# Two plain units of weights instead of three after each block of seven products

## The chip, the cores and the metric

One core of a Trainium2 chip runs the whole kernel. The metric is the device time of one execution in microseconds; three runs of the kernel before were timed, and one execution was profiled.

## The reference

A decoder trunk of two layers over 256 tokens of width 2048, in float32. Layer 0 mixes tokens with stick-breaking attention, layer 1 with a gated DeltaNet; a SwiGLU feed-forward of hidden width 5632 follows each. The change lies in the feed-forward alone:

```python
D_MODEL = 2048; SEQ = 256; DEPTH = 2; FFN_HIDDEN = 5632

def swiglu(h, w_gu, w_down):
    gate, up = jnp.split(h @ w_gu, 2, axis=-1)
    return (jax.nn.silu(gate) * up) @ w_down

for i in range(DEPTH):
    x = x + mixer(rms_norm(x, mix_norm[i]))          # mixer by layer
    x = x + swiglu(rms_norm(x, ffn_norm[i]), ffn_w_gu[i], ffn_w_down[i])
```

## The kernel before

**Units.** Weights come from HBM in units of 256 rows by 512 columns (`Unit`, `UK = 2` tiles of 128 rows; one load of 512 KB). A unit belongs to a `Block`, which is 512 columns of a product with all its rows. TensorE multiplies in fp32r, so each operand is split in a high and a low part: ScalarE writes the high part (L328), VectorE subtracts it from the raw weights and writes the low part (L332). This is a unit's conversion. TensorE then makes three products for each tile (high by high, high by low, low by high; L354).

**Two kinds of unit in the feed-forward.** A *plain unit* needs 12 matmuls of 512 columns. Its conversion is one instruction of 1024 columns on ScalarE and one on VectorE; in the profile it is named `slabs<-slab`. The gate and up products of six of the eleven column groups (`SEVEN`) are made in a form of Strassen's method with seven products of half size instead of eight; such a *seven unit* needs 21 matmuls of 256 columns. VectorE first forms sums of quarters of the weights (`sums`: one instruction of 512 columns and two of 256, `w<-w`); its conversion is 1792 columns on ScalarE and on VectorE, for every second one in two pieces of 768 and 1024 (`w<-w,w`). A block of seven products has eight seven units, and twelve such blocks (gate and up in turn) make 96 seven units in a layer; I number them 1 to 12.

**The end of such a block.** The results lie in four PSUM banks, `acc` two times and `bank` two times, which the next block of seven products uses again. They are drained by `quarters`: one ScalarE copy (`slab<-acc`, 256 columns) and four VectorE additions (`slab<-acc,slab` and `slab<-bank,slab`). Behind a gate block ScalarE applies silu; behind an up block VectorE multiplies gate and up (`slab<-slab,rstd`), transposes twice (L939), and transfers through HBM finish the transposition. Plain blocks (the other column groups, and the down projection) use the remaining banks; theirs are products with `rstd` from a bank, transposes, and additions into `x`.

**Buffers.** Plain units have two raw and two converted buffers, seven units three raw and two converted ones (each then converted alternately in one and in two pieces). A converted buffer is free when TensorE has finished the unit in it. Conversions are written into the engines' queues in the order of the units, up to three units ahead (`AHEAD`), sums up to five ahead (`SUMS`).

**The order.** `ffn_units` makes the lists of the seven units and of the plain ones; the first 13 plain units stand first (`LEAD + BEFORE`), and `merge` finds the order of the rest, 96 seven and 155 plain ones, as the cheapest path through all orders by costs: for a seven unit that follows the end of a block of seven products with `gs` plain units between, for two seven units in a row, for more than three plain ones in a row, and for a distance from 1.3 plain units to each seven unit (`RATIO`). `gs` counts up to three. The resulting order sets the queue of every engine, TensorE's first; a planner in the program (`tick`, `spend`) lets the smaller tasks (drains, silu, transposes) into the queues by its own account of times. Then each engine works through its queue in order and waits on semaphores.

Of the kernel before, what the change touches and what calls it, by code (L numbers as in the profile page):

```python
# [157 lines left out]
class Trunk:  # L158
# [867 lines left out]
    def merge(self, s, o):  # L1026


        ns, no = len(s), len(o)
        ends = [u.last for u in s]  # L1030
        best = {(0, 0, 0, 1, 3): (0.0, None)}
        layer = best
        trail = []
        for _ in range(ns + no):
            nextl = {}
            for st, (cost, _p) in layer.items():
                i, j, kind, run, gs = st

                for k in (0, 1):
                    ii, jj = i + k, j + 1 - k  # L1040
                    if ii > ns or jj > no or (k and kind == 1 and run >= 2):
                        continue
                    c = cost
                    if k:
                        c += 4.0 * max(0, 2 - gs) + (1.0 if gs == 2 else 0)
                        c += 0.3 * (kind == 1)
                        g2 = 0 if ends[i] else 3
                    else:
                        g2 = min(3, gs + 1)
                    r = min(run + 1, 4) if k == kind else 1  # L1050
                    if not k and r > 3 and ii < ns:
                        c += 2.0
                    if ii < ns:
                        c += 0.15 * max(0.0, abs(jj - self.RATIO * ii) - 1.5)
                    key = (ii, jj, k, r, g2)
                    if key not in nextl or nextl[key][0] > c:
                        nextl[key] = (c, st)
            trail.append(nextl)
            layer = nextl
        st = min(layer, key=lambda q: layer[q][0])  # L1060
        order = []
        for nextl in reversed(trail):
            order.append(st[2])
            st = nextl[st][1]
        return order[::-1]
# [727 lines left out]
```

## Time and profile before

| | |
|---|---|
| runs | 2709.22, 2709.37, 2713.18 us (median 2709.37) |
| profiled execution | 2705.98 us, span 2704.3 us |
| granted TensorE clock | 1.000 |
| read from HBM, over the span | 508.20 MB, 197 GB/s read and written |
| seven units, layer 0 (plain ones between them) | about 440 to 1037 us of the span |
| seven units, layer 1 | about 2020 to 2619 us |

In the profile PE is TensorE's matmul, PEld its weight load, DVE VectorE, ACT ScalarE, SP the engine that issues the loads. A row of a timeline gives the start in us from the span's start, the length in us (of equal neighbours merged, with their count), engine, line, operation, what is written and read, and in brackets the idle time before it and who ended it. A row of windows gives for each engine the busy time and the number of instructions.

### The profile page before, as it was taken

Reading aid. Unit: us, or ns where it says so; the run is one execution under the profiler, and the core shown is the slowest. Engines: PE = TensorE matmul, PEld = TensorE weight load, DVE = VectorE, ACT = ScalarE, POOL = GpSimd, SP = SyncE. Lnnn points to the kernel's source line nnn. Section 1 sums busy time; section 2 is a strip of 40 time slices with the busy share of each in tenths; the row PEclk is TensorE's granted clock in tenths of the full one; section 3 lists DMA queues with packets and bytes.
Section 4 is the critical chain, followed back from the end, with each engine's and each line's share of the span. In section 5 each row is a group of like instructions: output and inputs, shape, how many; then the busy total and the mean of one; then the engine's idle time right before and its main releaser. Section 6 shows DMA issues by size and latency. Waiting matters only on the chain.

```text
span 2704.3 us, 39527 instructions
## 1 busy us (share of the span) xinstructions
PE 2669.4 (99%) x14730; PEld 2274.6 (84%) x14730; DVE 2182.7 (81%) x3451; ACT 1491.8 (55%) x1961; POOL 11.2 (0%) x95
## 2 busy tenths in 40 slices
PE   9999999999999999999999999999999999999999
PEld 7888888888888888888888888888878888888887
DVE  6556568899999897678778887887679899989885
ACT  6555556554555554565665556645575555555453
POOL 0000000000000000000000000000000000000000
PEclk9999999999999999999999999999999999999999
DMA  7766775787676777855656556556567767767776
GB/s 245 202 185 196 219 211 164 208 231 212 203 218 205 208 211 233 227 174 172 182 143 195 159 161 175 168 153 186 170 191 212 223 196 220 217 188 218 226 209 188
DMA packets 487611, 534.41 MB, mean 198 GB/s; under 512 B 188087, under 2 KB 267258, under 8 KB 487418
## 3 DMA queue, kind: packets, MB, share of 16 engines
q1 hardware_dynamic: 487370, 531.87, 67.1%
q8 instruction: 115, 1.88, 0.3%
q14 instruction: 78, 0.64, 0.1%
q10 hardware_dynamic: 48, 0.02, 0.0%
HBM read 508.20 MB, written 23.59 MB: 197 GB/s over the span
## 4 chain that ended last, share of the span: by engine, by line
PE 83%; DVE 10%; issue 2%; ACT 2%; DMA 2%; SPq 0%; ACTq 0%; DVEq 0%
PE acc L354 61%; PE bank L354 20%; DVE w L332 5%; DVE slabs L332 2%; PE bank L363 1%; DMA slab<-in_ffn_w_gu_dram 1%; ACT slabs L328 1%; ACT w L328 1%; DVE slab L338 1%; DVE slab L332 1%; DVE slab L939 1%; DMA slab<-in_ffn_w_down_dram 0%; ACT slab L328 0%; DVE x L332 0%; DMA w<-in_ffn_w_gu_dram 0%
## 5 line engine op out<-in xcount | busy, mean ns | idle before, releaser
L332 DVE TENSOR_TENSOR w<-w,w 128x1024 fp32r<-128x1024 f32 (+2 forms) x746 | 946.3, 1285 | 249.0 <-ACT w L328 247.6
L328 ACT ACTIVATE w<-w 128x1024 fp32r<-128x1024 f32 (+2 forms) x650 | 802.8, 1244 | 417.8 <-PE acc L354 347.0
L354 PE MATMUL acc<-w,hTh 128*128 128x512 f32 (+1 forms) x3232 | 925.0, 369 | 9.1 <-DVE w L332 8.4
L354 PEld LDWEIGHTS acc<-w,hTh 128*128 128x128 f32 x3232 | 585.9, 189 | 120.5 <-DVE w L332 14.5
L354 PE MATMUL acc<-w,hTl 128*128 128x512 f32 (+1 forms) x1616 | 590.2, 365 | 3.1 <-DVE hTl L338 3.1
L328 ACT ACTIVATE slabs<-slab 128x1024 fp32r<-128x1024 f32 x264 | 279.3, 1058 | 431.9 <-DMA slab<-in_ffn_w_gu_dram 123.8
L332 DVE TENSOR_TENSOR slabs<-slab,slabs 128x1024 fp32r<-128x1024 f32 x264 | 321.5, 1218 | 93.1 <-ACT slabs L328 93.1
L354 PE MATMUL acc<-w,kh 128*128 128x512 f32 x1184 | 369.6, 393 | 0.0
L354 PEld LDWEIGHTS acc<-w,hTl 128*128 128x128 f32 x1616 | 304.5, 188 | 53.5 <-DVE hTl L338 3.9
L332 DVE TENSOR_TENSOR w<-w 128x256 f32<-128x256 f32 (+1 forms) x576 | 291.2, 508 | 9.8 <-DMA w<-in_ffn_w_gu_dram 2.6
L354 PEld LDWEIGHTS acc<-w,kh 128*128 128x128 f32 x1184 | 218.8, 188 | 43.7
L354 PE MATMUL acc<-w,kl 128*128 128x512 f32 x592 | 230.7, 390 | 0.0
L354 PE MATMUL acc<-slabs,hTh 128*128 128x512 f32 x608 | 190.1, 392 | 2.8 <-DVE slabs L332 2.8
L354 PE MATMUL bank<-w,wide 128*128 128x256 f32 x1296 | 178.9, 283 | 0.0
L354 PEld LDWEIGHTS bank<-w,wide 128*128 128x128 f32 x1296 | 165.8, 192 | 0.0
L354 PE MATMUL bank<-slabs,hTh 128*128 128x512 f32 x512 | 159.9, 392 | 3.1 <-DVE slabs L332 3.1
L354 PE MATMUL bank<-slabs,kh 128*128 128x512 f32 x512 | 159.6, 392 | 3.4 <-DVE slabs L332 3.4
L354 PE MATMUL acc<-slabs,kh 128*128 128x512 f32 x480 | 149.9, 392 | 2.1 <-DVE slabs L332 1.9
L354 PEld LDWEIGHTS acc<-slabs,hTh 128*128 128x128 f32 x608 | 111.0, 188 | 25.1 <-DVE slabs L332 4.9
L354 PEld LDWEIGHTS acc<-w,kl 128*128 128x128 f32 x592 | 111.1, 188 | 23.4
L354 PE MATMUL acc<-slabs,hTl 128*128 128x512 f32 x304 | 118.3, 389 | 0.0
L328 ACT ACTIVATE slab<-bank 32x128 f32<-32x128 f32 (+4 forms) x181 | 67.9, 379 | 89.3 <-PE bank L354 87.1
(216 smaller groups left out, 2933.4 us busy)
## 6 DMA issues: line engine op xcount, KB each, us to landing
w<-in_ffn_w_gu_dram SPq DMA_DIRECT2D x212, 512.0 KB, 4.5
slab<-in_ffn_w_gu_dram SPq DMA_DIRECT2D x140, 512.0 KB, 4.5
w<-in_gdn_w_in_dram SPq DMA_DIRECT2D x129, 512.0 KB, 4.3
slab<-in_ffn_w_down_dram SPq DMA_DIRECT2D x124, 512.0 KB, 4.5
w<-in_sb_w_in_dram SPq DMA_DIRECT2D x96, 512.0 KB, 4.5
w<-in_gdn_w_in_dram SPq DMA_DIRECT2D x128, 256.0 KB, 3.7
w<-in_gdn_w_out_dram SPq DMA_DIRECT2D x64, 512.0 KB, 4.4
w<-in_ffn_w_down_dram SPq DMA_DIRECT2D x52, 512.0 KB, 5.5
```

The costliest lines, as they stand in the source:

```text
L328: self.nc.scalar.activation(out, in_, func, **kw)
L332: self.nc.vector.tensor_tensor(out, a, b, op=op)
L338: self.nc.vector.scalar_tensor_tensor(out, a, s, b, op0=op0, op1=op1)
L354: self.nc.tensor.matmul(out, lhsT, rhs, start=start, stop=stop, skip_group_check=True)
L363: self.nc.tensor.transpose(out, in_, self.ident[:p, :p])
L939: self.nc.vector.transpose(s, t)
```

## The change

```diff
@@ -1042,7 +1042,7 @@ merge
                     c = cost
                     if k:
-                        c += 4.0 * max(0, 2 - gs) + (1.0 if gs == 2 else 0)
+                        c += 4.0 * max(0, 2 - gs)
                         c += 0.3 * (kind == 1)
                         g2 = 0 if ends[i] else 3
```

A seven unit after exactly two plain units behind a block's end no longer costs anything. In the order that `merge` finds, with p a plain and s a seven unit, the blocks 2 to 6 then read (blocks 1 and what follows 12 are as before):

```text
block  before               after
2      pppspspspspspspsps   ppsppspspsppspspsps
3      pppspspsppspspspsps  ppspspsppspspspsps
4      pppspspspspspspsps   ppsppspspspsppspsps
5      pppspspsppspspspsps  ppspspsppspspspsps
6      pppspspspspspspsps   ppspsppspspspspsps
```

All eleven blocks from 2 to 12 begin with three plain units before and with two after, in both layers; the third is found later in the block. The numbers of both kinds of unit are the same.

Two places show what this does to the queues. First VectorE at the end of block 2 in layer 0, before: the row of `slabs` with 1024 columns is a plain conversion (here that of the third plain unit of block 3), the one with 1792 columns the conversion of the first seven unit of block 3, the rows with `acc_104`, `bank_108` and `bank_110` are the drain.

```order
L338 SCALAR_TENSOR_TENSOR slab<-acc_106,rstd_141,slab 128x512
L338 SCALAR_TENSOR_TENSOR slab<-acc_107,rstd_141,slab 128x512
L332 TENSOR_TENSOR w_2928<-w_2928 128x512
L332 TENSOR_TENSOR slab<-acc_104,slab 128x512
L332 TENSOR_TENSOR w_2928<-w_2928 128x256
L332 TENSOR_TENSOR slab<-bank_108,slab 128x512
L332 TENSOR_TENSOR w_2928<-w_2928 128x256
L332 TENSOR_TENSOR slab<-bank_110,slab 128x2x256
L332 TENSOR_TENSOR slab<-bank_108,slab 128x256
L939 STREAM_TRANSPOSE slab<-slab 128x512 x2
L332 TENSOR_TENSOR slabs<-slab,slabs 128x1024
L332 TENSOR_TENSOR w_123<-w_122,w_123 128x1792
```

The same place after; the first `slabs` row is now the conversion of the second plain unit of block 3, the last that of the third.

```order
L332 TENSOR_TENSOR slabs<-slab,slabs 128x1024
L332 TENSOR_TENSOR w_2928<-w_2928 128x256 x2
L332 TENSOR_TENSOR w_123<-w_122,w_123 128x1792
L332 TENSOR_TENSOR slab<-acc_104,slab 128x512
L332 TENSOR_TENSOR slab<-bank_108,slab 128x512
L332 TENSOR_TENSOR slab<-bank_110,slab 128x2x256
L332 TENSOR_TENSOR slab<-bank_108,slab 128x256
L332 TENSOR_TENSOR w_122<-w_122 128x512
L332 TENSOR_TENSOR slabs<-slab,slabs 128x1024
L332 TENSOR_TENSOR w_122<-w_122 128x256 x2
L332 TENSOR_TENSOR w_123<-w_2928,w_123 128x768
L332 TENSOR_TENSOR w_2927<-w_122,w_123 128x1024
```

The conversion of the first seven unit stood behind the drain and the third plain conversion; now it stands ahead of the drain, and the third plain conversion behind it. The two products with `acc_106` and `acc_107` and the two transposes, of a plain up block that ends there, have moved up, ahead of the second plain conversion.

On ScalarE the same place reads before as follows (the 256 columns of `acc_105` are the drain's copy):

```order
L328 ACTIVATE w_123<-w_122 128x1792
L328 ACTIVATE slabs<-slab 128x1024 x2
L328 ACTIVATE slab<-acc_105 128x256
L328 ACTIVATE slabs<-slab 128x1024
L328 ACTIVATE w_123<-w_122 128x1792
```

and after:

```order
L328 ACTIVATE w_123<-w_122 128x1792
L328 ACTIVATE slabs<-slab 128x1024 x2
L328 ACTIVATE w_123<-w_122 128x1792
L328 ACTIVATE slab<-acc_105 128x256
L328 ACTIVATE slabs<-slab 128x1024
```

The conversion of the first seven unit has passed the drain's copy and the third plain conversion.

The second place is VectorE at the end of block 6, before, from the drain's last addition on:

```order
L332 TENSOR_TENSOR slab<-bank_108,slab 128x256
L332 TENSOR_TENSOR slabs<-slab,slabs 128x1024
L332 TENSOR_TENSOR w_123<-w_122,w_123 128x1792
L338 SCALAR_TENSOR_TENSOR slab<-slab,rstd_141 128x512 x2
L332 TENSOR_TENSOR w_2928<-w_2928 128x512
L332 TENSOR_TENSOR slabs<-slab,slabs 128x1024
L332 TENSOR_TENSOR w_2928<-w_2928 128x256
L332 TENSOR_TENSOR x_63<-bank_111,x_63 128x512
L332 TENSOR_TENSOR w_2928<-w_2928 128x256
L332 TENSOR_TENSOR x_63<-bank_109,x_63 128x512
```

and after, from the same addition on:

```order
L332 TENSOR_TENSOR slab<-bank_108,slab 128x256
L332 TENSOR_TENSOR slabs<-slab,slabs 128x1024
L332 TENSOR_TENSOR w_2928<-w_2928 128x512
L332 TENSOR_TENSOR slabs<-slab,slabs 128x1024
L332 TENSOR_TENSOR w_2928<-w_2928 128x256
L332 TENSOR_TENSOR x_63<-bank_111,x_63 128x512
L332 TENSOR_TENSOR w_2928<-w_2928 128x256
L332 TENSOR_TENSOR x_63<-bank_109,x_63 128x512
L338 SCALAR_TENSOR_TENSOR slab<-slab,rstd_141 128x512 x2
L332 TENSOR_TENSOR w_123<-w_122,w_123 128x768
```

Here the first seven unit's conversion is gone from behind the drain (it is ahead of it), and sums, additions and gate products now stand between the drain and the second seven unit's conversion.

## The prediction

> **What bounds the kernel now.** I read the page first, then busy time by stretches, then the waits of the engines, then the timeline of one place.
>
> ```profile
> span 2704.3 us, 39527 instructions
> PE 2669.4 (99%) x14730; PEld 2274.6 (84%) x14730; DVE 2182.7 (81%) x3451; ACT 1491.8 (55%) x1961; POOL 11.2 (0%) x95
> ```
>
> TensorE is busy all the time, so a new order of the same products can only win back the gaps between them. The next view shows the two stretches that the change reorders (blocks 2 to 12 of the seven products, in either layer), and two single blocks, 3 and 4.
>
> ```profile
> core 0: us, PE busy (x) PEld busy (x) DVE busy (x) ACT busy (x) POOL busy (x), PEclk, DMA share, GB/s
> 486.00:1037.00 551.00, 542.98 (x3239) 481.99 (x3237) 502.83 (x637) 291.81 (x253) 0.00 (x0) 1.00 0.72 210
> 2066.00:2618.00 552.00, 543.36 (x3238) 481.87 (x3238) 502.98 (x637) 292.69 (x255) 0.00 (x0) 1.00 0.72 210
> 534.00:586.00 52.00, 50.40 (x299) 44.43 (x298) 48.16 (x63) 28.35 (x26) 0.00 (x0) 1.00 0.82 226
> 586.00:634.00 48.00, 48.00 (x294) 43.10 (x292) 45.14 (x58) 25.29 (x21) 0.00 (x0) 1.00 0.67 205
> ```
>
> Here VectorE is nearly as full as TensorE: 502.83 of 551 us. TensorE has no gap in block 4 (48.00 of 48) and gaps in block 3 (50.40 of 52). How much is lost in all I take from starts, since a matmul's shown end hides part of a gap. These rows, from TensorE's timeline, are the first matmuls of an eighth seven unit: of blocks 1, 3, 4 and 12 in the first layer, 1 and 12 in the second.
>
> ```profile
> 483.19 0.40 PE L354 MATMUL acc<-w,hTh 128*128 128x256 f32 x2
> 583.73 0.40 PE L354 MATMUL acc<-w,hTh 128*128 128x256 f32 x2
> 631.25 0.40 PE L354 MATMUL acc<-w,hTh 128*128 128x256 f32 x2
> 1034.73 0.40 PE L354 MATMUL acc<-w,hTh 128*128 128x256 f32 x2
> 2063.43 0.40 PE L354 MATMUL acc<-w,hTh 128*128 128x256 f32 x2
> 2615.90 0.40 PE L354 MATMUL acc<-w,hTh 128*128 128x256 f32 x2
> ```
>
> Block 4, without a gap, takes 631.25 - 583.73 = 47.52 us for 8 seven and 10 plain units. From block 1 to block 12 there are 88 seven and 116 plain units, which is 11 such blocks and 6 plain units more; at 2.75 us for a plain unit (below) that is 11 x 47.52 + 16.5 = 539.2 us. Measured are 551.5 and 552.5 us. So 12.3 + 13.3 = 25.6 us are lost in gaps, and that is the most the change can win.
>
> The Trainium skill (Trainium Kernel Development and Optimization, Performance Expectations) calls matmul busy time a bad measure, because matmuls are pipelined, and weight-load busy time a good one. The trace agrees: by PE busy the two stretches lose only (551 - 542.98) + (552 - 543.36) = 16.7 us, which would cap the gain there; but block 3's weight loads at block 4's rate (43.10 / 48) leave 52 - 44.43 / 0.898 = 2.5 us free, where PE busy shows 1.6.
>
> What ends the gaps is seen at the end of block 2 (time E = 533.85). TensorE, first the eighth seven unit, then the first plain unit, the second, and the second matmul of the third:
>
> ```profile
> 531.34 0.40 PE L354 MATMUL acc<-w,hTh 128*128 128x256 f32 x2
> 533.85 0.63 PE L354 MATMUL bank<-slabs,hTh 128*128 128x512 f32 x2
> 536.60 0.62 PE L354 MATMUL bank<-slabs,hTh 128*128 128x512 f32 x2
> 541.28 0.50 PE L354 MATMUL bank<-slabs,hTh 128*128 128x512 f32 x1 [1.57 <-DVE slabs L332]
> ```
>
> A seven unit takes 2.51 us, a plain one 2.75, and the third plain unit stops for its low part. VectorE at the same place:
>
> ```profile
> 525.32 2.10 DVE L332 TENSOR_TENSOR w<-w,w 128x768 fp32r<-128x768 f32 x2 [1.83 <-ACT w L328]
> ...
> 532.63 1.23 DVE L332 TENSOR_TENSOR slabs<-slab,slabs 128x1024 fp32r<-128x1024 f32 x1 [3.15 <-ACT slabs L328]
> 533.77 0.42 DVE L332 TENSOR_TENSOR w<-w 128x256 f32<-128x256 f32 x1
> 534.11 1.40 DVE L338 SCALAR_TENSOR_TENSOR slab<-acc,rstd,slab 128x512 f32<-128x512 f32 x2
> 535.43 0.68 DVE L332 TENSOR_TENSOR w<-w 128x512 f32<-128x512 f32 x1
> 536.03 0.69 DVE L332 TENSOR_TENSOR slab<-acc,slab 128x512 f32<-128x512 f32 x1
> ...
> 537.89 1.01 DVE L332 TENSOR_TENSOR slab<-bank,slab 128x512 f32<-128x512 f32 x2
> 538.83 1.29 DVE L939 STREAM_TRANSPOSE slab<-slab 128x512 f32<-128x512 f32 x2
> 540.04 1.18 DVE L332 TENSOR_TENSOR slabs<-slab,slabs 128x1024 fp32r<-128x1024 f32 x1
> 541.15 2.01 DVE L332 TENSOR_TENSOR w<-w,w 128x1792 fp32r<-128x1792 f32 x1
> 543.08 0.68 DVE L332 TENSOR_TENSOR w<-w 128x512 f32<-128x512 f32 x1
> 543.68 1.22 DVE L332 TENSOR_TENSOR slabs<-slab,slabs 128x1024 fp32r<-128x1024 f32 x1
> 544.82 0.42 DVE L332 TENSOR_TENSOR w<-w 128x256 f32<-128x256 f32 x1
> 545.15 0.74 DVE L338 SCALAR_TENSOR_TENSOR slab<-slab,rstd 128x512 f32<-128x512 f32 x1
> ...
> 546.81 2.09 DVE L332 TENSOR_TENSOR w<-w,w 128x768 fp32r<-128x768 f32 x2
> 548.82 1.22 DVE L332 TENSOR_TENSOR slabs<-slab,slabs 128x1024 fp32r<-128x1024 f32 x1
> ```
>
> VectorE stands idle for 1.83 and 3.15 us just before E, and then has no pause until the gap. Why it idles is in ScalarE's timeline and in VectorE's waits over the first stretch:
>
> ```profile
> 531.54 1.06 ACT L328 ACTIVATE slabs<-slab 128x1024 fp32r<-128x1024 f32 x1 [4.15 <-PE acc L354]
> 532.51 0.36 ACT L328 ACTIVATE slab<-acc 128x256 f32<-128x256 f32 x1
> 536.80 1.06 ACT L328 ACTIVATE slabs<-slab 128x1024 fp32r<-128x1024 f32 x1 [3.93 <-PE bank L354]
> 537.77 1.68 ACT L328 ACTIVATE w<-w 128x1792 fp32r<-128x1792 f32 x1
> ```
>
> ```profile
> DVE slabs L332 <- ACT slabs L328: 40.3, 29, 4.1
> ```
>
> Plain units have two converted buffers. With three plain units in a row ahead, the second can be converted only when the one before the eighth seven unit is done (531.54), the third only when the first is done (536.80), and the next seven unit's conversion stands behind that (537.77). So the two idle engines have nothing they may do before E, and after E everything comes at once. VectorE waits 40.3 us of the first stretch in this way.
>
> **The change, part by part.** No instruction and no byte is added or removed: per layer 96 seven and 168 plain units stay. Eleven block ends per layer change; block 1 and what follows block 12 do not.
>
> (a) The first seven unit of the next block comes one plain unit (2.75 us) earlier. Its conversion no longer stands behind the third plain unit's on ScalarE, so it falls into the idle time and stands ahead of the drain. I set up VectorE's queue at the end of block 2 with start-to-start times of the rows above: plain conversion 1.14, seven conversion 1.93 (as a pair 2.01), sums 0.60 and 2 x 0.40, drain 0.60 x 3 + 0.33 = 2.13, two gate products 1.34, two transposes 1.21. The second plain unit's conversion ends at E - 0.1 as now; on ScalarE the seven conversion follows it at once (E - 1.3 + 1.7 = E + 0.4). VectorE: sums to E + 0.7, seven conversion to 2.6, drain to 4.8, sums and third plain conversion to 7.3, second seven conversion to 9.3, gate products 10.7, fourth plain conversion 11.8, sums 13.3, third seven conversion 15.3. TensorE needs the drained banks and the first seven unit at 2 x 2.75 = 5.5, the third plain unit at 8.0, the second seven unit at 10.7, the fourth plain unit at 13.5 and the third seven unit at 16.0. Nothing is late. The gap of 1.7 us goes; next to be late is the third seven unit, 0.7 us ahead.
>
> (b) The same sum at the other ten ends. Late remain: the third seven unit of block 5 (two adds, 0.60 each as a piece of the drain, and two gate products stand before it) by 0.5; the second of block 6, where products of a plain block hold the conversion up to E + 3.9, by 0.45 in its second piece; the third of blocks 7 and 9 (products, then transposes) by 0.5 and 0.4. With about 0.1 us that a gap's next matmul loses, that is 2.3 us per layer. Ends 1 and 10 clear by less than 0.8 us; for these I add 0.9. So 3.2 per layer, 6.4 in both.
>
> (c) The plain unit that is taken from the end goes to later pairs of plain units in the block. Each spare one gives VectorE 2.75 - 1.14 = 1.6 us where it has no backlog now; I cost and credit it at nothing. Its cover is VectorE's lead there; a pair of a plain and a seven unit needs 1.14 + 1.97 + 1.40 = 4.5 of its 5.26 us, so if the lead were gone, a pair with two gate products would be short by 0.6 us.
>
> (d) The queue that issues the loads keeps the order within each kind; a seven unit's buffer is free when its conversion ends, now 541.15 + 1.93 = E + 9.2, after at E + 2.6, so those loads start earlier. Plain loads wait for the plain conversions as now. A transposed pair's transfers change place by at most a unit or two. I cost this at nothing; the cover is that the rows of VectorE's waits name ScalarE for 40.3 us there. Bounds: a gain of nothing, a loss of one late load of a unit's length (2.75 us) at a few ends, 8 us.
>
> Sum: -25.6 + 6.4 = -19.2 us. The profiled execution took 2705.98 us (span 2704.3), so 2686.8; the median of the runs is 3.4 us above it, 2709.37 - 19.2 = 2690.2 us.
>
> **The rivals.**
>
> 1. The gaps only move (same). VectorE has the same work, and block 3, for one, loses 583.73 - 531.34 - (47.52 + 2.75) = 2.1 us. With one plain unit fewer ahead of the first seven units VectorE would be short there instead. Against it: 551 - 502.83 = 48 us of idle VectorE time, most of it just before the ends. Time: 2709.
>
> 2. Part of it moves (faster, less). If every one of the 22 ends keeps about 0.7 us (my estimate, a third of the 2.1 us of block 3), the gain is 25.6 - 15.4 = 10 us: 2699.
>
> 3. The drain comes too late (slower). It now stands behind a seven conversion, and two plain units cover 5.5 us, not 8.2. In the ledger it ends at E + 4.8 to 6.0. If the second plain conversion is late by more than a microsecond, for a load or a product, the seven conversion, the drain and the first seven unit are late by as much, 22 times. It decides from 25.6 / 22 = 1.2 us of mean gap per end; at 1.6 us it gives 22 x 0.4 = 9 us more, 2718. For it: at 532.63 VectorE waits at the head of its queue while a ready sum stands behind. The Trainium skill (TensorE: Matmul & The Clock Gate, Architectural detail) says the same, VectorE and ScalarE are strict first-in first-out; by it the drain cannot pass a late conversion. Against: ScalarE took that conversion at 531.54 as soon as TensorE released it, so the load had long landed.
>
> **How the numbers follow.** The main case has 0.64, rival 2 0.18, rival 1 0.09, rival 3 0.09. About 0.2% (5.4 us) is what a measurement of this kernel tells from no change. Faster: 0.64 + 0.18 = 0.82; same 0.09; slower 0.09. The range goes from all gaps gone, 2709.4 - 25.6 = 2684, to rival 2 with its scatter, 2702 (its chance, the main case's, less tails: 0.8).
>
> **What would show it.** Right: TensorE's wait for the low part of the third plain unit after a block is gone; VectorE's wait for the plain conversions in the first stretch falls from 40.3 us to under 30; block 1 to block 12 takes about 542 us, from 551.5; the third seven unit of blocks 5, 7 and 9 still stops. Wrong: the first seven unit of a block stops on the drain or its conversion, or ScalarE waits for a load of a plain unit ahead of it.

## The result, and the profile after

| | before | after |
|---|---|---|
| runs, us | 2709.22 to 2713.18 (4) | 2694.69 to 2697.89 (4) |
| median, us | 2709.39 | 2695.55 |
| ratio | | 0.9947, 95% interval 0.9933 to 0.9962 |
| profiled execution, us | 2705.98 | 2695.05 |

The change made the kernel 13.8 us faster. The forecast was 19.2 us faster (2690.2); the measured time lies in its range of 2684 to 2702, 5.3 us above the forecast itself. The page of after:

```profile
span 2693.3 us, 39460 instructions
PE 2668.9 (99%) x14730; PEld 2277.9 (85%) x14730; DVE 2187.5 (81%) x3451; ACT 1489.5 (55%) x1961; POOL 11.2 (0%) x95
```

PE, PEld, DVE, ACT and POOL ran as many instructions as before, in a shorter span. Where it was won is read as before, from the first matmul of the eighth seven unit of blocks 1 and 12 in TensorE's timeline, in the first layer and the second:

```profile
483.01 0.40 PE L354 MATMUL acc<-w,hTh 128*128 128x256 f32 x2
1028.29 0.40 PE L354 MATMUL acc<-w,hTh 128*128 128x256 f32 x2
2060.22 0.40 PE L354 MATMUL acc<-w,hTh 128*128 128x256 f32 x2
2605.39 0.40 PE L354 MATMUL acc<-w,hTh 128*128 128x256 f32 x2
```

The stretches take 545.28 and 545.17 us, from 551.54 and 552.47. Against the 539.2 us without gaps, 6.1 + 6.0 = 12.1 us are left of 25.6. So 6.3 + 7.3 = 13.6 us were won, and the medians differ by 13.8. The two profiled spans differ by 11.0 only: between the stretches (from block 12 of the first layer to block 1 of the second) after takes 1031.93 us, before 1028.70, and those 3.2 us are the clock: matmul by matmul, after falls 1.6 us behind before over each of two stretches at half clock, and nowhere else there (last section).

The waits of TensorE's matmuls from 486 to 1031 us, all rows of the list, and the first row of VectorE's:

```profile
PE acc L354 <- DVE w L332: 2.7, 4, 0.9
PE bank L354 <- DVE slab L332: 0.5, 2, 0.3
PE bank L354 <- DVE w L332: 0.2, 1, 0.2
```

```profile
DVE slabs L332 <- ACT slabs L328: 35.0, 27, 3.8
```

TensorE's matmuls no longer wait for `slabs`, the low part of a plain unit. They wait for `w` (conversions of seven units) and for `slab` (the drain). VectorE's wait for plain conversions fell only from 40.3 to 35.0 us. The end of block 2 shows why; the block ends at E = 536.55 (its eighth seven unit starts at 534.04). VectorE, then ScalarE:

```profile
535.33 1.23 DVE L332 TENSOR_TENSOR slabs<-slab,slabs 128x1024 fp32r<-128x1024 f32 x1 [0.98 <-ACT slabs L328]
536.47 0.88 DVE L332 TENSOR_TENSOR w<-w 128x256 f32<-128x256 f32 x2
537.27 2.02 DVE L332 TENSOR_TENSOR w<-w,w 128x1792 fp32r<-128x1792 f32 x1
539.20 0.68 DVE L332 TENSOR_TENSOR slab<-acc,slab 128x512 f32<-128x512 f32 x1
539.92 1.75 DVE L332 TENSOR_TENSOR slab<-bank,slab 128x512 f32<-128x512 f32 x3
542.18 1.22 DVE L332 TENSOR_TENSOR slabs<-slab,slabs 128x1024 fp32r<-128x1024 f32 x1
...
550.10 2.02 DVE L332 TENSOR_TENSOR w<-w,w 128x1792 fp32r<-128x1792 f32 x1
```

```profile
534.24 1.06 ACT L328 ACTIVATE slabs<-slab 128x1024 fp32r<-128x1024 f32 x1 [4.15 <-PE bank L354]
535.21 1.69 ACT L328 ACTIVATE w<-w 128x1792 fp32r<-128x1792 f32 x1
```

The seven conversion starts at E + 0.7, as the forecast's sum had it, but that is not the idle time before E: it stands behind the second plain unit's conversion, for which ScalarE still waits 4.15 us until TensorE frees a buffer. The drain ends at E + 5.1 (539.92 + 1.75), and the first seven unit needs its banks from E + 5.5 on.

### The profile page after: what moved, and what is told of

It reads as the page before. It is cut to its first block, busy times and chain, and to the rows that moved or that the text cites. A ratio compares the mean times of both kernels' runs of the same rounds, so it can differ in the third digit from the quotient of the medians.

```text
span 2693.3 us, 39460 instructions
## 1 busy us (share of the span) xinstructions
PE 2668.9 (99%) x14730; PEld 2277.9 (85%) x14730; DVE 2187.5 (81%) x3451; ACT 1489.5 (55%) x1961; POOL 11.2 (0%) x95
## 4 chain that ended last, share of the span: by engine, by line
PE 82%; DVE 11%; DMA 2%; ACT 2%; issue 2%; ACTq 0%; SPq 0%; DVEq 0%
PE acc L354 60%; PE bank L354 21%; DVE w L332 6%; DVE slabs L332 3%; PE bank L363 1%; ACT slabs L328 1%; DVE slab L332 1%; DMA slab<-in_ffn_w_gu_dram 1%; DMA w<-in_ffn_w_gu_dram 1%; ACT w L328 1%; DMA slab<-in_ffn_w_down_dram 1%; DVE slab L338 0%; ACT slab L328 0%; DVE x L332 0%; DVE slab L939 0%
```

## The experiments

Each trial ran beside the kernel before on the same chip, in three batches (e1 to e4, e5 to e8, e9 and e10; medians of before 2710.39, 2709.85 and 2708.12 us). The table orders them by two things: how many plain units stand between a block's end and the next seven unit, and where that first seven unit is converted. "Gaps" is the sum over both layers of block 1 to block 12 less 539.2 us (less 536.45 us where only 115 plain units lie between), from the profiled execution. Half clock (last section) is in it: by half the length of its stretches in the trace about 34 us in e2_early, 15 in e10_one_ahead, 7 in e7_ahead3 and in e4_one, and none in the others.

| kernel | plain units | first seven unit converted | ratio to before | gaps, us |
|---|---|---|---|---|
| before | 3 | behind drain and third plain unit | 1 | 25.6 (e8_before: 29.0) |
| e2_early | 3 | behind the second plain unit, ahead of drain and third | 1.0197 [1.0179, 1.0216] | 84.8 |
| e7_ahead3 | 3 | ahead of the second plain unit | 1.0056 [1.0044, 1.0069] | 43.8 |
| e3_hold | 2 | behind the drain | 0.9970 [0.9958, 0.9982] | 18.6 |
| e1_swap_only | 2 | behind the second plain unit, ahead of the drain | 0.9963 [0.9951, 0.9976] | 16.8 |
| after | 2 | the same | 0.9947 [0.9933, 0.9962] | 12.1 |
| e5_late_up | 2 | the same | 0.9952 [0.9938, 0.9965] | 12.6 |
| e6_ahead2 | 2 | ahead of the second plain unit | 0.9905 [0.9892, 0.9919] | 1.4 |
| e9_swap_ahead | 2 | ahead of the second plain unit | 0.9902 [0.9886, 0.9917] | none (-0.2) |
| e4_one | mostly 1 | behind that plain unit | 1.0013 [1.0004, 1.0022] | 31.7 |
| e10_one_ahead | mostly 1 | ahead of the plain unit that follows it | 1.0070 [1.0057, 1.0083] | 48.9 |

**The exchange alone (e1_swap_only).** The order of before, with plain, plain, plain, seven behind an end turned into plain, plain, seven, plain, and nothing else moved:

```diff
-        return order[::-1]
+        order = order[::-1]
+        i = 0
+        for n, x in enumerate(order):
+            i += x
+            if x and ends[i - 1] and order[n + 1:n + 5] == [0, 0, 0, 1]:
+                order[n + 1:n + 5] = [0, 0, 1, 0]
+        return order
```

> The order of before, with one exchange at each end of a block of seven products: p p p s becomes p p s p, so the third plain unit stands right behind the first seven unit and is not carried further into the block. Theory A (the third plain unit gets its conversion due one seven unit later, and that is where the gain is): about all of the change's gain, 2692 to 2698 us, and about 12 us of gaps between block 1 and block 12 of both layers together, as in the changed kernel. Rival B (the gain comes from the spare plain units spread over the later block): only a part, 2700 to 2709 us.

Measured 2700.20 us (2697.55 to 2701.51), before 2710.39: 10.2 us faster. That is just inside rival B's range and 2 us above theory A's, and the gaps are 16.8 us where A had 12. The exchange by itself carries most of the gain: 10.2 of 13.8 us by the medians, 8.8 of 13.5 by the gaps. The rest is small against the noise, since the two intervals in the table overlap. The traces show where it lies: e1 loses 2.5 and 1.4 us in blocks 3 and 6 of the first layer, where after loses 0 and 0.8.

**The order of before, with the conversion moved alone (e2_early).** In the conversion loop, when a block's first seven unit is the one behind the next unit, it is converted first:

```diff
+                    while ahead < len(units) and units[ahead].conv is not None:
+                        ahead += 1
+                w = units[ahead + 1] if ahead + 1 < len(units) else None
+                if i < ahead and ahead + 1 <= i + self.AHEAD and w is not None and w.lane == "s" and w.first and w.conv is None:
+                    if self.may_convert(w):
+                        self.convert(w)
+                        self.pump()
```

> TensorE's order of before (three plain units), but the first seven unit of a block is converted ahead of the drain and of the third plain unit, as in the changed kernel. Theory A (TensorE's order gives the third plain unit its time): slower than before, since the third plain unit's conversion now ends 1.3 to 3.7 us late at each of the 22 ends; in all about 20 us of gaps per layer where before has 12 to 13, so 2720 to 2730 us. Rival C (as the forecast put it: the conversion ahead of the drain fills idle time, and that wins): faster, 2693 to 2700 us.

Measured 2765.54 us, 55 us slower. Theory A has the direction, but the time is 35 us beyond its range, about as much as the half clock takes (34 us). At the end of block 2 the third plain unit stands still for 4 us, and the clock is halved from the end of that gap on. TensorE's row and the window from there (columns as in the prediction; PEclk is the eighth figure, 0.50):

```profile
551.72 0.80 PE L354 MATMUL bank<-slabs,hTh 128*128 128x512 f32 x1 [4.01 <-DVE slabs L332]
```

```profile
550.90:557.70 6.80, 5.98 (x17) 4.92 (x18) 6.80 (x10) 0.88 (x1) 0.00 (x0) 0.50 0.67 179
```

So what before loses isn't lost because the seven conversion is late. With three plain units in a row, the third one's conversion is the urgent one, and the seven conversion put ahead of it costs TensorE time: TensorE stops at the third plain unit behind all 22 ends.

**The order of after, with the conversion held back (e3_hold).** The first seven unit is not converted before the drain of the block ahead of it is in the queue:

```diff
+                    v, o = units[ahead], self.owner[0]
+                    if v.lane == "s" and v.first and ahead > i and o is not None and o.kind == "seven" and not o.evacuated:
+                        break
```

> TensorE's order of the changed kernel, but the first seven unit of a block is converted only after the drain. Theory A: most of the gain stays; the drain ends about 1.5 to 2 us earlier and the conversion ends close to its due time, so 2695 to 2701 us, with the gaps at a block's first seven unit ended by its conversion instead of the drain. Rival C (the conversion ahead of the drain wins): most of the gain is lost, 2703 to 2710 us.

Measured 2702.11 us (2697.56 to 2704.57), 8.3 us faster than before, between the ranges of A and C. The waits of TensorE's matmuls from 486 to 1031 us have one row:

```profile
PE acc L354 <- DVE w L332: 6.2, 9, 1.2
```

Nine stops, all for conversions of seven units; the wait for `slabs` is gone here too. So the order removes the third plain unit's gap without the conversion ahead of the drain. What that place of the conversion adds is known less well: 18.6 - 12.1 = 6.5 us by the gaps (the profiled execution was the longest of the six), 13.8 - 8.3 = 5.5 us by the medians, with intervals that just overlap.

**One plain unit (e4_one).** The cost for one is taken away as well (`4.0 * max(0, 1 - gs)`), and most blocks then begin with one.

> The cost of one plain unit behind a block's end is taken away too, so that most blocks begin with one plain unit, some with two. Theory A and rival D (the drain's cover is what bounds, so that fewer plain units end in waits on the drain) differ: by A the drain, which ends about 2.6 us behind the end where the conversion is already done, is covered by one plain unit of 2.75 us, and the loss is the shortage of VectorE ahead of the second and third seven units, 2694 to 2704 us; by D each end waits about 1.5 us on the drain, 33 us in all, 2715 to 2735 us.

Measured 2714.06 us, 3.7 us slower than before, between the two ranges and next to D's. With one plain unit (2.75 us) as cover, the drain is late. TensorE's waits from 486 to 1031 us, the first two rows:

```profile
PE bank L354 <- DVE slab L332: 4.6, 7, 1.0
PE acc L354 <- DVE slab L332: 3.4, 3, 2.1
```

That is about 8 us in this stretch and as much in the other, half of what D had. Without the 7 us of half clock its gaps would be 25, as many as those of before.

**Later gate products (e5_late_up).** After, with one line that lets the gate products and transposes behind an up block into the queues 6 us later:

```diff
         def up(acc, free):
             duo = yield from self.quarters(acc, free)
+            self.cur.later = 6.0
             yield
```

> The changed kernel, with the gate products and transposes behind an up block of seven products let into the queues 6 us later by the program's planner; no work is left out. Theory A (the gaps that the change left come from small work standing ahead of the third seven unit's conversion on VectorE): the gaps of the third seven units of blocks 5, 7, 9 and 11 go (3.3 us in layer 0, about 3 in layer 1 by the trace of after), and the time is about 2689 to 2692 us. Theory D (what is left comes from late loads and late transposed data ahead of the drain): the third units' gaps go but the first units' stay, 2693 or more; theory M (the gaps only move): the products come late where the next plain block needs them, and the time is 2695 or above.

Measured 2696.66 us, the same as after. TensorE's waits over the same stretch show the exchange:

```profile
PE bank L354 <- DVE slab L332: 2.6, 5, 0.8
PE acc L354 <- DVE w L332: 0.5, 1, 0.5
PE bank L354 <- DVE w L332: 0.2, 1, 0.2
```

The third seven units' 2.7 us fell to 0.5, and the first seven units' wait for the drain rose from 0.5 to 2.6. The gaps moved, and the time is in the range of theory M (and of D, whose first units were to stay as they were). They did not move in the way that M gives. Later products mean later transposes and later transposed data, and the conversion of these (`kl<-slab,kh`) now comes when a block ends. VectorE at the end of block 5, E = 683.67:

```profile
687.52 1.29 DVE L332 TENSOR_TENSOR kl<-slab,kh 128x512 fp32r<-128x512 f32 x2
688.72 0.68 DVE L332 TENSOR_TENSOR slab<-acc,slab 128x512 f32<-128x512 f32 x1
```

In after the same conversion ran at 678.16, 4.5 us before that end; here it stands directly ahead of the drain. At the ends of blocks 3, 9 and 11 it is late too; at the fifth stop, behind block 6, a plain load is. The small work ahead of the third seven unit did make the gap there, but what depends on that work makes another when it is moved.

**The conversion ahead of the one that waits (e6_ahead2).** After, with a block's first seven unit converted ahead of the second plain unit's conversion. It needs no plain buffer to come free, only its own (lines left out at `...`):

```diff
-                while ahead < min(i + self.AHEAD, len(units)) and self.may_convert(units[ahead]):
+                while ahead < min(i + self.AHEAD, len(units)):
+                    for w in units[ahead + 1:i + 3 + 1]:
+                        if w.lane == "s" and w.first and w.conv is None and units[ahead].lane == "b" and self.may_convert(w):
+                            self.convert(w)
+                            self.pump()
+                    if not self.may_convert(units[ahead]):
+                        break
...
                     ahead += 1
                     self.pump()
+                    while ahead < len(units) and units[ahead].conv is not None:
+                        ahead += 1
```

> The changed kernel, with the first seven unit of a block converted ahead of the second plain unit's conversion, so that it needs no buffer to come free and can run in the idle time before the end of a block; no work is left out. Theory E (the idle time before the end, about 5 us per end, is what the change leaves unused, and filling it wins most of the gaps that are left): gaps of about 1 to 3 us per layer instead of 6.3 and 6.1, the time 2684 to 2690 us, and VectorE's wait for plain conversions in the first stretch falls from 35.0 to under 25 us. Theory C (what the first seven unit is put ahead of becomes late): the second plain unit's conversion comes 1.9 us later and stops TensorE for 0.5 to 1 us at many ends; 2698 to 2710 us. The trial of the kernel before with such a conversion ahead of the drain was 1.0197 times before, which speaks for C; but there the third plain unit paid, which here comes later.

Measured 2683.81 us (2682.78 to 2685.23), before 2709.85: 26.0 us faster, a little more than theory E gave. In the first stretch TensorE's matmuls have no wait in the list, and 0.1 us is lost. VectorE at the end of block 2, which ends at 533.91 + 2.51 = 536.42:

```profile
535.05 2.02 DVE L332 TENSOR_TENSOR w<-w,w 128x1792 fp32r<-128x1792 f32 x1
536.99 1.22 DVE L332 TENSOR_TENSOR slabs<-slab,slabs 128x1024 fp32r<-128x1024 f32 x1
538.12 0.69 DVE L332 TENSOR_TENSOR slab<-acc,slab 128x512 f32<-128x512 f32 x1
538.85 1.74 DVE L332 TENSOR_TENSOR slab<-bank,slab 128x512 f32<-128x512 f32 x3
541.11 1.22 DVE L332 TENSOR_TENSOR slabs<-slab,slabs 128x1024 fp32r<-128x1024 f32 x1
```

The seven conversion starts at E - 1.4 instead of E + 0.7, the drain ends at E + 4.2 instead of E + 5.1, and the third plain conversion begins 0.9 us earlier as well (E + 4.7, from E + 5.6). The second plain conversion, now behind it, is in time. Theory E's sign was missed even so: VectorE's wait for plain conversions is 28.3 us from 486 to 1025 us, not under 25, so much idle time stays; what counts is that the seven conversion and the drain come earlier.

**The same with three plain units (e7_ahead3).** The same lines in the kernel before (with a reach of four units instead of three):

> The kernel before, three plain units after each block's end, with the first seven unit of the next block converted ahead of the second plain unit's conversion; no work is left out. Theory A (the third plain unit in a row is what must be late, since its conversion waits for the first one's buffer): the third plain unit still stops, 0.5 to 2 us at most ends, now with the seven conversion ahead of it: 2705 to 2725 us. Theory E (early conversion is what counts, the number of plain units does not): the gaps fall to 4 to 5 us per layer, 2693 to 2697 us, the same as the changed kernel.

Measured 2724.49 us, 14.6 us slower than before, at the upper edge of theory A's range. The same edit that wins 12 us on top of two plain units loses 15 with three. TensorE's waits, first stretch:

```profile
PE bank L354 <- DVE slabs L332: 9.2, 7, 2.5
PE acc L354 <- DVE slabs L332: 4.7, 3, 2.1
```

Eight of these ten stops are again for the low part of the third plain unit behind an end.

**The kernel before once more (e8_before).**

> The kernel before, unchanged, profiled a second time. If the 3.4 us between its first profiled execution (2705.98) and its median (2709.4) are stretches of half clock that come in some executions, a profile near 2709 shows one or two such stretches of 3.4 us with a granted clock below 1 where the first shows none, each costing 1.6 us; a profile near 2706 shows none. If the two are not connected, a profile near 2709 shows none either and is longer elsewhere. The gaps between the blocks of seven products should be 12.3 and 13.3 us again, to 0.3 us.

Measured 2711.67 us at a mean clock of 1.000: a time above the median without any half clock to explain it, and gaps of 13.9 and 15.1 us, so the expectation was wrong in its first reading and in the gaps. Against its first profile, 2.3 us lie ahead of the first stretch (block 1's eighth seven unit at 485.53, from 483.19) and 3.4 us in the two stretches (553.07 and 554.30 us). The gaps of one kernel vary by a few us between executions, and a gain that is read from one pair of profiles is known to about that. One profile does not settle the first question, however. Of the 34 timed runs of before beside the experiments, the 7 with a granted clock of 1.000 took 2706.2 to 2708.2 us, the 20 with 0.999 took 2706.5 to 2711.3, and the 7 with 0.998 took 2710.6 to 2713.5: most of their scatter goes with the clock, as first supposed, and this profile is an exception.

**The early conversion with the exchange alone (e9_swap_ahead),** that is, the lines of e6 in the kernel of e1:

> The kernel before with the third and the first exchanged at every end of a block of seven products (plain, plain, seven, plain instead of plain, plain, plain, seven; all else in the order of before), and with the first seven unit of a block converted ahead of the second plain unit's conversion; no work is left out. Its twin without the early conversion took 2700.2 us, and lost in blocks 3 and 6, where a plain block ends at the same place. Theory E (the idle time before the end is what matters, and where the third plain unit goes does little once it is used): gaps of at most 2 us per layer, 2683 to 2688 us. Theory P (the places that the path found for the third plain unit matter by themselves): blocks 3 and 6 keep about 1 us each and some 3 to 5 us per layer stay, 2690 to 2696 us.

Measured 2682.74 us (2681.12 to 2684.69), before 2708.12: 25.4 us faster, and as fast as e6. Windows of blocks 2 to 12, both layers, then VectorE's first wait in the first:

```profile
486.00:1025.00 539.00, 539.00 (x3241) 482.57 (x3241) 500.78 (x635) 291.87 (x252) 0.00 (x0) 1.00 0.70 214
2056.00:2595.00 539.00, 539.00 (x3242) 482.69 (x3241) 500.75 (x635) 291.51 (x253) 0.00 (x0) 1.00 0.70 214
```

```profile
DVE slabs L332 <- ACT slabs L328: 23.9, 24, 2.7
```

TensorE is busy 539.00 of 539 us, and VectorE's wait for plain conversions is at 23.9 us. No gap is left, so where the third plain unit goes no longer matters once the seven conversion is early.

**One plain unit with the early conversion (e10_one_ahead),** the lines of e6 in the kernel of e4:

> One plain unit between the end of most blocks of seven products and the next seven unit (the cost for one removed as well), with the first seven unit of a block converted ahead of the plain unit that follows it; no work is left out. Without the early conversion this order took 2714.1 us. The drain takes 2.1 us on VectorE and 0.36 on ScalarE ahead of it, the one plain unit covers 2.75 us. Theory G (what counts is that VectorE is free when the block ends; then one plain unit is enough): the first seven unit stops at most 0.3 us, gaps of 2 to 4 us per layer, 2686 to 2692 us. Theory H (two plain units are needed, since the drain's start is late by what VectorE has in hand at the end): the first seven unit stops 0.5 to 1.5 us at the ends with one plain unit, 2697 to 2715 us.

Measured 2730.03 us, 21.9 us slower than before and 15 us beyond theory H, about what the half clock takes. VectorE and TensorE at the end of block 2, which ends at 540.89 + 2.51 = 543.4:

```profile
545.73 1.21 DVE L332 TENSOR_TENSOR slabs<-slab,slabs 128x1024 fp32r<-128x1024 f32 x1
546.86 0.42 DVE L332 TENSOR_TENSOR w<-w 128x256 f32<-128x256 f32 x1
547.19 0.68 DVE L332 TENSOR_TENSOR slab<-acc,slab 128x512 f32<-128x512 f32 x1
```

```profile
547.93 0.50 PE L354 MATMUL acc<-w,hTh 128*128 128x256 f32 x2 [0.72 <-DVE slab L332]
549.59 0.50 PE L354 MATMUL bank<-w,hTh 128*128 128x256 f32 x2 [1.04 <-DVE slab L332]
```

As in e4 at the same end, a second plain conversion stands ahead of the drain, which begins at E + 3.8 (E + 3.5 in e4) where one plain unit covers 2.75. So the early conversion does not bring the drain forward here.

## Why the prediction was right, and where not

*The bound.* That gaps of 25.6 us are all there is to win held to the end: e9 has no gap and is 25.4 us faster than before. That the two agree to 0.2 us is partly luck, since the second profile of before has 29.0 us of gaps. The check of the two busy measures on block 3 decides nothing: by starts the block lost 2.1 us, midway between 1.6 by PE busy and 2.5 by weight loads. Over both stretches 25.4 us were won in e9 where PE busy showed 16.7.

*Part (a)* was right in its sums (but for the fourth plain unit, due at E + 13.3, not 13.5): at the end of block 2 the drain ended at E + 5.1 (forecast 4.8), the third plain conversion at 543.3 (542.18 + 1.14), E + 6.8 (7.3), the third seven conversion began at 550.10, E + 13.5 (13.3). The third plain unit's gap is gone. Its words were wrong: the seven conversion does not fall into the idle time, since on ScalarE the second plain conversion still stands ahead of it. Nor is that conversion the main source of the gain: in e3 it stays behind the drain, and 8.3 of the 13.8 us are still won by the order. Its place is why the sign "under 30 us" failed at 35.0, and where the 12 us lie that e6 won.

*Part (b)* is the term that was mis-sized: 6.4 us of remaining gaps, measured 12.1. The four named gaps are there, and larger. With what the next matmul loses, the third seven unit of block 5 stops for 0.82 us, the second of block 6 for 0.75, the third of 7 and 9 for 0.99 and 0.77: 3.3 us in the first layer, forecast 2.3. Behind ends 1 and 10, in blocks 2 and 11, 2.2 us are lost there, allowed were 0.9. Another 0.8 us lie behind end 6, which the sum took as clear; that is a load's (part d). The largest single one is the third seven unit of block 11. TensorE, and ahead of it VectorE:

```profile
949.06 0.39 PE L354 MATMUL acc<-w,hTh 128*128 128x256 f32 x1 [0.89 <-DVE w L332]
```

```profile
945.46 0.71 DVE L939 STREAM_TRANSPOSE slab<-slab 128x512 f32<-128x512 f32 x1
946.39 0.70 DVE L939 STREAM_TRANSPOSE slab<-slab 128x512 f32<-128x512 f32 x1
947.02 1.98 DVE L332 TENSOR_TENSOR w<-w,w 128x1792 fp32r<-128x1792 f32 x1
```

*Part (d)* was wrong in its cover. Loads were costed at nothing because VectorE's waits named ScalarE. But such a wait is handed on from engine to engine: ScalarE waits for a plain load, the second plain conversion is late, and with it everything behind. The end of block 1, ScalarE, VectorE, TensorE:

```profile
484.30 1.06 ACT L328 ACTIVATE slabs<-slab 128x1024 fp32r<-128x1024 f32 x1 [3.75 <-DMA slab<-in_ffn_w_gu_dram]
```

```profile
488.05 2.02 DVE L332 TENSOR_TENSOR w<-w,w 128x1792 fp32r<-128x1792 f32 x1
490.70 1.74 DVE L332 TENSOR_TENSOR slab<-bank,slab 128x512 f32<-128x512 f32 x3
```

```profile
492.18 0.50 PE L354 MATMUL bank<-w,hTh 128*128 128x256 f32 x2 [0.32 <-DVE slab L332]
```

This is rival 3 in small, by the very sign that the prediction named. In after the first seven unit waits for the drain at four of the 22 ends, two in each layer: behind a late load at the two of the first layer, behind a late transposed pair and behind other work on VectorE in the second. In e6 the seven conversion no longer stands behind the second plain one, and no first seven unit waits for the drain in either stretch.

*The rivals.* By size the result lies between the main case (2690) and rival 2 (2699), a little nearer the latter. By mechanism it is the main case with a piece of rival 3. Rival 1, gaps that only move, is what e5 did to those that the change had left.

*What stays open.* That a third converted plain buffer would remove the gaps of before as well, which its waits suggest, was not tried. Why e4 and e10 draw half clock where after does not was not followed up either.

## What to carry to other kernels

When two engines are idle just ahead of a crowded moment, ask which of the queued instructions could start soonest, and put that one first; moving work "earlier" won most here where it passed the instruction that is itself waiting (e6, 12 us more than after). An order and a queue position must be judged together: here the same early conversion was worth -12 us with two plain units and +15 with three. A gap that remains behind small work need not be cured by moving that work: in e5 the work that depends on it came later too, and made a gap at the next drain.

## What was not expected of the hardware

In two stretches of 3.4 us the profiled execution of after had half the TensorE clock, one in layer 1's mixer, one just behind a gap. The windows (PEclk 0.50), the gap, and the same gap in before with its window, at full clock:

```profile
1540.80:1544.20 3.40, 3.40 (x11) 2.52 (x10) 1.24 (x10) 3.27 (x8) 0.00 (x0) 0.50 0.75 225
1984.60:1988.00 3.40, 3.40 (x9) 2.65 (x8) 3.40 (x6) 3.27 (x8) 0.00 (x0) 0.50 0.52 163
```

```profile
1983.60 0.50 PE L354 MATMUL acc<-w,hTl 128*128 128x512 f32 x1 [1.53 <-DVE hTl L338]
```

```profile
1988.41 0.50 PE L354 MATMUL acc<-w,hTl 128*128 128x512 f32 x1 [1.53 <-DVE hTl L338]
```

```profile
1985.00:1995.00 10.00, 8.43 (x40) 6.51 (x40) 9.79 (x22) 9.87 (x21) 0.00 (x0) 1.00 0.55 155
```

At half clock 3.4 us do the work of 1.7, and the lag of after behind before grows by 1.6 us over each: two such stretches are the 3.2 us that after lost between its two feed-forwards. Ahead of the first of them there was no gap: TensorE was busy for all of the 10.80 us from 1530 on. The Trainium skill (TensorE: Matmul & The Clock Gate, What's actually happening) tells of a free-running window of 3413 ns; the stretches have that length (3.41 us in the trace's clock record), and one and the same gap of 1.53 us led to half clock in one execution and not in the other. In e2 the gaps of up to 4 us were followed by such stretches at many ends (PEclk 0.97 on average over either stretch of 582 us, about 17 us each if TensorE was busy in them): there, gaps of that size cost more than their own length.
